# The first norm's weight in PSUM, two weights split on GpSimd, and a wider set of PSUM banks for the attention's transposes

## The chip, the cores and the metric

The kernel runs on one core of a Trainium2 chip. The metric is the device time of one execution in microseconds (us). TensorE (PE in the profile) multiplies matrices and transposes; its weight loads are listed apart (PEld). VectorE (DVE), ScalarE (ACT) and GpSimd (POOL) work elementwise, and SyncE (SP) issues the DMAs here. TensorE writes PSUM, which has eight banks; a bank holds 128 x 512 fp32 values.

## The reference

The reference is a two-layer encoder trunk on 1024 positions of width 1024. Layer 0 mixes tokens by attention with a forget gate, layer 1 by a state-space model; each is followed by a SwiGLU layer, and every part has an RMS norm before and after it. The change touches the very first norm, the projections behind it and the attention. Cut to these:

```python
def rmsnorm(x, gain):
    y = xf * lax.rsqrt(jnp.mean(xf * xf, axis=-1, keepdims=True) + EPS)
    return (y * gain.astype(jnp.float32)).astype(x.dtype)
...
    h = rmsnorm(x, mix_pre_gain[i])
...
def fox_mixer(h, w_in, b_f, q_gain, k_gain, w_out):
    proj = h @ w_in                       # q, k, v, gate, forget logits
    q = rmsnorm(heads(q), q_gain); k = rmsnorm(heads(k), k_gain)
    c = jnp.cumsum(log_sigmoid(f_logit + b_f), axis=1)
    for blk in range(seq_len // Q_BLOCK): # 8 query blocks of 128
        s = q_blk @ k[:k_end].T * scale + c_q - c_k     # 16 heads
        p = softmax(where(mask, s, -inf))
        outs.append(p @ v[:k_end])
    return (o * sigmoid(gate)) @ w_out
```

## The kernel before

Every matrix product is made of three fp32r products: each operand is split into a high part (a cast) and a low part (the difference), and `mm3` (L272 to L274) issues high x high, low x high and high x low. The program is written in an order, and a planner lays out each engine's instructions at compile time from estimated times and priorities; it adds the waits. The order of each engine is then fixed. Tiles in SBUF lie on numbered pages; a ring (`R("x")`) hands its pages out in turn, and a transfer into a page waits until the page's last user is done.

*The start.* SP issues, in this order, block 0 of the input (128 positions x 1024, 512 KB), the norm's weight vector spread over 128 partitions (`gain`, L338, also 512 KB, from one row of 4 KB), blocks 1 to 3, the first two weight tiles of the projections (512 KB each), and blocks 4 to 7. Input blocks use a ring of six pages, so blocks 6 and 7 wait for blocks 0 and 1. `first_norm` takes the blocks in turn. `norm` has ScalarE square and sum the block (L295) and take a root (L299); four small VectorE instructions (L301 to L304) make the reciprocal root. Even blocks are then multiplied by root and weight in one VectorE instruction (L318). Odd blocks are multiplied by the weight on GpSimd (blocks 1 and 3 ahead of the root, L311; blocks 5 and 7 after it, L315) and scaled there (L316). `to_fm` transposes the block on TensorE into two banks (L326, four transposes each), ScalarE casts the high part out of PSUM (L328), VectorE subtracts for the low part (L329). Blocks 0 to 3 are the first half of the positions.

`fox` weaves the rest of the first norm (blocks 4 to 7) with the first head pair's projections in `qkv`: the generators say how much work a step holds, and `weave` takes the one that is behind. The first projection, `qk_proj` of the query weight on the first half, needs blocks 0 to 3 and runs through `fm`, which goes over eight pieces k and yields after four. The first two weights are cast by ScalarE (L253) and subtracted by GpSimd (L254), both behind block 3's scaling; later weights are subtracted by VectorE.

*Attention.* `attend` goes over units: 16 heads, and in each the query blocks 7 down to 0. For a unit, `scores` multiplies into a slot of two PSUM banks (banks 0 and 1, or 2 and 3, in turn by unit; L551, L552). Block qb has (qb + 1) x 128 keys, so blocks 0 to 3 use the slot's first bank alone. VectorE adds the bias and takes the minimum (L555), ScalarE takes the exponential into SBUF (L561). `transposes`, one unit later, transposes the probabilities (L588) in groups of up to four 128 x 128 pieces: a first group for every block (front), a second for blocks 4 to 7 (rear). All groups go to one bank:

```python
PTB = (2,)          # pb() adds 4: PSUM bank 6
...
                p2 = self.pb(PTB, (P, 4, P))
```

ScalarE casts each group (L591) and VectorE subtracts (L592). `values` (L607) multiplies two query blocks at a time. Meanwhile the next head pair's projections (L272 to L274) fill TensorE; `weave` mixes the two streams.

Of the kernel before, what the change touches and what calls it, by code (L numbers as in the profile page):

```python
# [9 lines left out]
F32 = mybir.dt.float32  # L10
# [4 lines left out]
P = 128  # L15
D = 1024
# [10 lines left out]
PROJ = (0, 1)  # L27
# [4 lines left out]
PTB = (2,)  # L32
# [126 lines left out]
class Trunk:  # L159
    def __init__(self, ctx, tc, A, out):  # L160
        self.tc, self.nc, self.A, self.out = tc, tc.nc, A, out
        nc = self.nc
        mk = lambda name, bufs, **k: ctx.enter_context(tc.tile_pool(name=name, bufs=bufs, **k))
        self.cst = mk("cst", 1)
        self.hp = mk("hp", 4)
        self.pp = mk("pp", 1)
        self.sm = mk("sm", 4)
        self.sq = mk("sq", 1)
        self.ps = mk("ps", 1, space=bass.MemoryType.PSUM).tile([P, 8 * 512], F32, name="ps")
        self.nS, self.slots = 0, (0, 2)  # L170
        self.dr = mk("dr", 1, space=bass.MemoryType.DRAM)
        self.uid = 0
        self.R = Rings(tc, self.pp, NPG)
        self.R.set(raw=[0, 1, 2], wh=[3, 4], wl=[5, 6])
        self.B = {}
        c = self.cst
        self.ident = c.tile([P, P], F32, name="ident")
        make_identity(nc, self.ident)
        nc.scalar.preload_act_table_set("sqrt_and_others")
        self.eps = c.tile([P, 1], F32, name="eps")  # L180
        nc.vector.memset(self.eps, EPS)
        self.one = c.tile([P, 1], F32, name="one")
        nc.vector.memset(self.one, 1.0)
        self.lsub, self.proj = nc.vector, PROJ
        self.W, self.loaded, self.cut, self.taken, self.done = [], [], [], 0, {None}

    def nm(self, s):
# [62 lines left out]

    def split(self, h, l, src):
        with self.tc.high_priority(-100):
            self.nc.scalar.copy(h, src)  # L253
            self.lsub.tensor_sub(l, src, f32(h))  # L254

    def take(self, ahead=1):
# [16 lines left out]
        mm(ps, lh, rl, start=False, stop=False)  # L273
        mm(ps, ll, rh, start=False, stop=stop)  # L274

    def fm(self, ps, w, hT, half, step=4):
        wh, wl = w
        h, l = hT[half]
        for k in range(8):
            self.mm3(ps, wh[:, k, :], wl[:, k, :], h[:, k, :], l[:, k, :], k == 0, k == 7)  # L280
            if k % step == step - 1:
                yield 0.65 * step
# [118 lines left out]
        nc.vector.tensor_tensor_scan(z, ones, t1, 0.0, op0=ALU.mult, op1=ALU.add)  # L401
        nc.sync.dma_start(self.csum, z)

    def qk_proj(self, w, hT, hf, st):
        nc = self.nc
        if "p" not in st:
            st["p"] = [self.R(f"p{i}", dt=F32R) for i in st["pages"]]
        ps = self.pb(self.proj)
        yield from self.fm(ps, w, hT, hf)
        X, Y = st[hf] = self.R("pt", (P, 2, 512)), self.R("pt", (P, 2, 512), F32R)  # L410
        with self.tc.high_priority(AHEAD):
            nc.scalar.copy(X[:, 1], ps)
            nc.vector.tensor_mul(X[:, 0], X[:, 1], X[:, 1])
        nc.scalar.copy(Y[:, 0], X[:, 0])
        nc.vector.tensor_sub(Y[:, 1], X[:, 0], f32(Y[:, 0]))
# [54 lines left out]
    def qkv(self, hT, res, hp):  # L470


        v = []
        a, f, b = self.qkp if hp else ([9, 11, 8], [7, 35, 10], [12, 13, 14])
        q, k = dict(pages=a + f[2:]), dict(pages=f[:2])
        self.qkp = a[:2] + f[:1], b, [a[2], f[2], f[1]]
        if hp == 0:
            self.lsub = self.nc.gpsimd
            with self.tc.issue_after(self.poolop.ins):
                wq, wk = self.take(), self.take(0)  # L480
            self.lsub = self.nc.vector
            yield from self.qk_proj(wq, hT, 0, q)
            yield from self.qk_proj(wk, hT, 0, k)
            yield from self.forget_logits(hT)
            yield from self.qk_proj(wq, hT, 1, q)
            self.proj = (0, 1, 2, 3)
            with self.tc.issue_after(self.sqrt.ins):
                self.nc.scalar.preload_act_table_set(LNEXP)
            self.forget_sum()
            yield from self.qk_norm(0, 0, q)  # L490
            yield from self.qk_proj(wk, hT, 1, k)
            wv = self.take()
            yield from self.qk_norm(1, 0, k)
            yield from self.qk_norm(0, 1, q)
        else:
            wk = self.take()
            yield from self.qk_proj(wk, hT, 0, k)
            yield from self.qk_proj(wk, hT, 1, k)
            wq = self.take()
            yield from self.qk_norm(1, 0, k)  # L500
            yield from self.qk_proj(wq, hT, 0, q)
            yield from self.qk_norm(1, 1, k)
            yield from self.qk_proj(wq, hT, 1, q)
            wv = self.take()
            yield from self.qk_norm(0, 0, q)
        last = self.qk_norm(0, 1, q) if hp else self.qk_norm(1, 1, k)
        yield from self.v_proj(wv, hT, v, last)
        res.update(q=q["p"], k=k["p"], v=v)
# [20 lines left out]
    def attend(self, c, o):  # L529
# [3 lines left out]

        nc = self.nc
        units = [(h, qb) for h in range(NH) for qb in reversed(range(8))]
        An, pt, Pt, pv, rs, ri = {}, {}, {}, {}, {}, {}

        def load_bias(h):
            An[h] = self.R("An")
# [2 lines left out]
        def scores(h, qb):  # L542
            qh, ql = c[h // 2]["q"][h % 2 * 2:h % 2 * 2 + 2]
            k = c[h // 2]["k"][h % 2]
            nk = (qb + 1) * P
            qs = slice(qb * P, nk)
            nc.gpsimd.tensor_add(An[h][:, qs], An[h][:, qs], self.cmask)  # L547
            ps = self.S("S")
            for c0 in range(0, nk, 512):
                c1 = min(c0 + 512, nk)  # L550
                nc.tensor.matmul(ps[:, c0:c1], qh[:, qs], k[:, c0:c1], start=True, stop=False)  # L551
                nc.tensor.matmul(ps[:, c0:c1], ql[:, qs], k[:, c0:c1], start=False, stop=True)  # L552
            with self.tc.high_priority(AHEAD):
                m = self.small("mx")
                nc.vector.tensor_tensor_reduce(out=ps[:, :nk], in0=ps[:, :nk], in1=An[h][:, :nk], op0=ALU.add, op1=ALU.min,  # L555
                                               scale=1.0, scalar=3e38, accum_out=m)
            p = Pt[h, qb] = self.R("Pt")
            if h // 2 not in rs:
                rs[h // 2] = self.small("rs", (P, 2, 8))
            r = rs[h // 2][:, h % 2, qb:qb + 1]  # L560
            nc.scalar.activation(p[:, :nk], ps[:, :nk], AF.Exp, bias=m, scale=-1.0, accum_out=r)  # L561
            if h >= NH - 2:
                nc.vector.reciprocal(r, r)
                nc.gpsimd.tensor_scalar(p[:, :nk], p[:, :nk], r, 1.0, op0=ALU.mult, op1=ALU.mult)
# [11 lines left out]
        def transposes(h, qb):  # L576
            j, qq = qb // 2, qb % 2
            if qq:
                ng = (2 * j + 2 + 3) // 4
                pt[h, j] = [(self.R("pth", (P, 4, 256), F32R), self.R("ptl", (P, 4, 256), F32R)) for _ in range(ng)]  # L580
            p = Pt.pop((h, qb))
            for g in range(0, qb + 1, 4):
                n = min(4, qb + 1 - g)
                if g:
                    yield 0.11 * 4
                p2 = self.pb(PTB, (P, 4, P))
                for i in range(n):
                    nc.tensor.transpose(p2[:, i], p[:, (g + i) * P:(g + i + 1) * P], self.ident)  # L588
                th, tl = pt[h, j][g // 4]
                dh, dl = th[:, 0:n, qq * P:qq * P + P], tl[:, 0:n, qq * P:qq * P + P]  # L590
                nc.scalar.copy(dh, p2[:, 0:n])  # L591
                nc.vector.tensor_sub(dl, p2[:, 0:n], f32(dh))  # L592
# [24 lines left out]
        for i in range(len(units) + 3):  # L617
            hp = min(i, len(units) - 1) // 16
            if i < len(units):
                h, qb = units[i]  # L620
# [6 lines left out]
            if 1 <= i <= len(units):  # L627
                h, qb = units[i - 1]
# [5 lines left out]
            if i >= 3 and (i - 3) % 2 == 1:  # L634
                h, qb = units[i - 3]
# [887 lines left out]
def trunk(ctx: ExitStack, tc: tile.TileContext, A, out):  # L1523
    T = Trunk(ctx, tc, A, out)
    nc, R = T.nc, T.R
# [36 lines left out]
    for f in range(8):  # L1562
        T.plan(T.cols(A["s5_w_glu"][0], f * P)[:3] + (("glu",) * 2 if f == 0 else (None,) * 2))
        if f >= 1:
# [7 lines left out]
                gn=[21, 22], ogk=[32])  # L1572
# [9 lines left out]
    hT = T.new_hT()  # L1582
    g0 = []

    def first_norm(tbs, banks):
        for tb in tbs:
            T.norm(xs[tb], g0[0], ys[tb], tb % 2 == 1, R("j") if tb in (1, 3) else None)
            T.to_fm(ys[tb], T.hT_dst(hT, tb), banks)
            yield 1.0

    xs, ys = {}, {}
    R.set(j=[36, 37])
    for tb in range(8):
        xs[tb], ys[tb] = R("x"), R("y")
        nc.sync.dma_start(xs[tb], x0[tb * P:tb * P + P, :])
        if tb == 0:
            g0.append(T.gain("gn", A["mix_pre_gain"][0]))
        if tb == 3:
            T._load(0)
            T._load(1)  # L1600
    T.fox_setup()
    run(first_norm(range(0, 4), (0, 1, 2, 3)))
    T.fox(hT, og_d, first_norm(range(4, 8), (2, 3)), OUT0)
# [9 lines left out]
    ys = {}  # L1613
# [90 lines left out]
```

## Time and profile before

| | |
|---|---|
| median of 3 runs | 2428.12 us (2426.31 to 2430.02) |
| profiled execution | 2426.33 us |
| its span, first to last instruction | 2424.5 us |
| mean granted TensorE clock | 0.995 |
| TensorE busy | 2359.3 us, 97% of the span |
| VectorE, ScalarE, GpSimd busy | 1689.1, 1204.4, 455.2 us |

A row of the timeline reads: start, duration, engine, line of the kernel, operation, output<-input, count; in brackets the idle time of the engine before it and what ended it. A row of a group reads: line, engine, operation, shapes and count | busy us, mean ns of one | idle us before, by releaser. TensorE's instructions are pipelined, and the profile models their ends: matmuls of 512 columns start 0.23 us apart and are listed as 0.39 us long.

### The profile page before, as it was taken

To read this page: it belongs to the slowest core of one execution; us is meant where nothing else is said; L and a number is where in the kernel's file an instruction comes from. 1 tells how busy PE (TensorE), PEld (TensorE's weight loads), DVE (VectorE), ACT (ScalarE), POOL (GpSimd) and SP (SyncE) were. 2 spreads that over 40 slices of the span, in tenths; PEclk is the share of its full clock that TensorE was granted. 3 is DMA by queue.
4 is the path that set the end of the run, shared out by engine and by line. 5 is a ranking of instruction groups with operands and counts; after the bars stand their busy time and mean duration, and the time that the engine had idled before them with its cause. 6 is when DMAs were issued, how large, how long until landed. Compare 5 with 4: busy or idle time off the path is not lost.

```text
span 2424.5 us, 31559 instructions
## 1 busy us (share of the span) xinstructions
PE 2359.3 (97%) x11683; PEld 1938.8 (80%) x11683; DVE 1689.1 (70%) x2684; ACT 1204.4 (50%) x2029; POOL 455.2 (19%) x427
## 2 busy tenths in 40 slices
PE   7999999999999999999999999999999999999997
PEld 5777778777777888888878779888878888888886
DVE  6867776677678967666668686763795656555867
ACT  6766676667646333434564563232453333333334
POOL 4222222222400034545520001410000000000003
PEclk9999999999999999999999999999999999999999
DMA  4121112121243444343688752443424333237874
GB/s 146 48 61 53 49 48 62 53 61 54 87 149 101 121 127 135 117 136 116 204 293 301 270 170 84 135 147 107 135 80 135 107 98 109 92 118 261 284 239 157
DMA packets 252427, 318.23 MB, mean 131 GB/s; under 512 B 34225, under 2 KB 179937, under 8 KB 252273
## 3 DMA queue, kind: packets, MB, share of 16 engines
q1 hardware_dynamic: 252272, 316.23, 40.9%
q8 instruction: 91, 1.49, 0.3%
q14 instruction: 64, 0.52, 0.1%
HBM read 238.46 MB, written 77.72 MB: 130 GB/s over the span
## 4 chain that ended last, share of the span: by engine, by line
PE 74%; DVE 12%; ACT 7%; DMA 3%; issue 3%; POOL 0%; SPq 0%; DVEq 0%; ACTq 0%; POOLq 0%
PE ps L841 33%; PE ps L943 10%; PE ps L272 7%; PE ps L274 7%; PE ps L273 7%; PE ps L588 2%; PE ps L607 2%; DVE ps L555 1%; DMA raw<-in_ffn_w_down_dram 1%; DMA rot_d<-ry 1%; ACT wh L253 1%; PE ps L552 1%; PE ps L551 1%; DVE ptl L592 1%; DVE y L318 1%
## 5 line engine op out<-in xcount | busy, mean ns | idle before, releaser
L841 PE MATMUL ps<-B,ah 128*128 128x512 f32 x1056 | 326.0, 390 | 0.3 <-ACT B L89 0.3
L943 PE MATMUL ps<-wdh,gh 128*128 128x512 f32 x616 | 241.4, 392 | 6.3 <-ACT m L962 3.7
L943 PE MATMUL ps<-wdh,gl 128*128 128x512 f32 x616 | 240.9, 391 | 1.9 <-DVE gl L254 1.9
L943 PE MATMUL ps<-wdl,gh 128*128 128x512 f32 x616 | 240.9, 391 | 0.8 <-DVE wdl L254 0.8
L841 PEld LDWEIGHTS ps<-B,ah 128*128 128x128 f32 x1056 | 198.1, 188 | 42.7 <-ACT B L89 1.2
L841 PE MATMUL ps<-ops,ah 128*128 128x512 f32 x704 | 218.2, 391 | 0.0
L272 PE MATMUL ps<-hT,wh 128*128 128x512 f32 x512 | 207.5, 406 | 1.3 <-DVE pt L429 0.7
L841 PE MATMUL ps<-B,al 128*128 128x512 f32 x528 | 205.4, 389 | 0.0
L273 PE MATMUL ps<-hT,wh 128*128 128x512 f32 x512 | 204.4, 399 | 0.0
L274 PE MATMUL ps<-hT,wl 128*128 128x512 f32 x512 | 202.6, 396 | 0.0
L253 ACT CAST gh<-gr 128x1024 fp32r<-128x1024 f32 (+1 forms) x78 | 81.1, 1040 | 166.4 <-PE ps L943 138.0
L592 DVE TENSOR_TENSOR ptl<-ps,pth 128x512 fp32r<-128x512 f32 x192 | 106.4, 554 | 78.6 <-ACT pth L591 73.6
L254 DVE TENSOR_TENSOR gl<-gr,gh 128x1024 fp32r<-128x1024 f32 (+1 forms) x78 | 98.3, 1262 | 84.0 <-ACT gh L253 83.7
L841 PEld LDWEIGHTS ps<-ops,ah 128*128 128x128 f32 x704 | 131.5, 188 | 28.7 <-issue 1.7
L812 DVE TENSOR_TENSOR al<-raw,ah 128x1024 fp32r<-128x1024 f32 x88 | 117.1, 1333 | 50.5 <-ACT ah L811 50.5
L1655 POOL TENSOR_TENSOR y<-m,s 128x512 f32<-128x512 f32 x4 | 6.5, 1628 | 764.3 <-DVE wdl L254 759.5
L547 POOL TENSOR_TENSOR An<-An,cmask 128x128 f32<-128x128 f32 x128 | 80.2, 629 | 365.8 <-DVE mx L555 332.3
L811 ACT CAST ah<-raw 128x1024 fp32r<-128x1024 f32 x88 | 92.6, 1052 | 101.8 <-PE ps L841 99.4
L943 PEld LDWEIGHTS ps<-wdh,gh 128*128 128x128 f32 x616 | 116.3, 189 | 32.8 <-ACT m L962 4.2
L943 PEld LDWEIGHTS ps<-wdh,gl 128*128 128x128 f32 x616 | 116.2, 189 | 26.9 <-DVE gl L254 2.7
L841 PE MATMUL ps<-ops,al 128*128 128x512 f32 x352 | 136.9, 389 | 0.0
L943 PEld LDWEIGHTS ps<-wdl,gh 128*128 128x128 f32 x616 | 116.3, 189 | 25.5 <-DVE wdl L254 1.5
(358 smaller groups left out, 5867.2 us busy)
## 6 DMA issues: line engine op xcount, KB each, us to landing
raw<-in_ffn_w_down_dram SPq DMA_DIRECT2D x98, 512.0 KB, 5.2
gr<-g_d SPq DMA_DIRECT2D x76, 512.0 KB, 4.4
raw<-in_ffn_w_gate_dram SPq DMA_DIRECT2D x44, 512.0 KB, 4.1
raw<-in_ffn_w_up_dram SPq DMA_DIRECT2D x44, 512.0 KB, 4.8
g_d<-s SPq DMA_DIRECT2D x66, 256.0 KB, 2.2
raw<-in_fox_w_in_dram SPq DMA_DIRECT2D x32, 512.0 KB, 4.3
g_d<-up SPq DMA_DIRECT2D x22, 512.0 KB, 2.7
g_d<-up SPq DMA_DIRECT2D x44, 256.0 KB, 2.9
```

What stands on the lines that cost most here:

```text
L253: self.nc.scalar.copy(h, src)
L254: self.lsub.tensor_sub(l, src, f32(h))
L272: mm(ps, lh, rh, start=start, stop=False)
L273: mm(ps, lh, rl, start=False, stop=False)
L274: mm(ps, ll, rh, start=False, stop=stop)
L547: nc.gpsimd.tensor_add(An[h][:, qs], An[h][:, qs], self.cmask)
L588: nc.tensor.transpose(p2[:, i], p[:, (g + i) * P:(g + i + 1) * P], self.ident)
L592: nc.vector.tensor_sub(dl, p2[:, 0:n], f32(dh))
L811: nc.scalar.copy(h, src)
L812: V.tensor_sub(l, src, f32(h))
L841: nc.tensor.matmul(bank, x[:, k], y, start=start and k == i == 0, stop=True, skip_group_check=True)
L943: nc.tensor.matmul(bank, x[:, j, t], y[:, j], start=start and i == 0, stop=True, skip_group_check=True)
```

## The change

At the start, a 4 KB row of the norm's weight is loaded first. TensorE spreads it: a matmul of a column of ones (one row, `ones`) with the row, twice 512 columns in fp32, writes it to all partitions of PSUM banks 0 and 1 (`gps`). Blocks 0 to 4 and 6 are multiplied by VectorE with the weight from PSUM. Blocks 5 and 7 stay on GpSimd, now with the multiply ahead of the root, and use the old spread tile, which is loaded after block 5. The second weight tile is loaded after block 5 as well. The first two weights are cast and subtracted on GpSimd, no longer behind a norm's instruction. The first projection runs with `apart`: eight high x high products, then eight low x high, then eight high x low, with a yield after each eight.

In attention, the rear groups, and the groups of blocks 2 and 3, go to the second bank of the slot that the unit's own scores used; the front groups of blocks 7 to 4, 1 and 0 stay in bank 6.

```diff
-        self.lsub, self.proj = nc.vector, PROJ
+        self.lsub, self.hcopy, self.proj = nc.vector, nc.scalar.copy, PROJ
...
     def split(self, h, l, src):
         with self.tc.high_priority(-100):
-            self.nc.scalar.copy(h, src)
+            self.hcopy(h, src)
             self.lsub.tensor_sub(l, src, f32(h))
...
+        if apart:
+            for n, (a, b) in enumerate(((wh, h), (wl, h), (wh, l))):
+                for k in range(8):
+                    self.nc.tensor.matmul(ps, a[:, k, :], b[:, k, :], start=n == k == 0, stop=n == 2 and k == 7)
+                yield 0.65 * 8 / 3
+            return
...
         if hp == 0:
-            self.lsub = self.nc.gpsimd
-            with self.tc.issue_after(self.poolop.ins):
-                wq, wk = self.take(), self.take(0)
-            self.lsub = self.nc.vector
-            yield from self.qk_proj(wq, hT, 0, q)
+            self.lsub, self.hcopy = self.nc.gpsimd, self.nc.gpsimd.tensor_copy
+            wq, wk = self.take(), self.take(0)
+            self.lsub, self.hcopy = self.nc.vector, self.nc.scalar.copy
+            yield from self.qk_proj(wq, hT, 0, q, True)
...
             ps = self.S("S")
+            own[h, qb] = self.slots[self.nS % len(self.slots)] + 1
...
-            p = Pt.pop((h, qb))
+            p, b = Pt.pop((h, qb)), own.pop((h, qb))
...
-                p2 = self.pb(PTB, (P, 4, P))
+
+                p2 = self.bank(b, 1, (P, 4, P)) if g or qb in (2, 3) else self.pb(PTB, (P, 4, P))
...
     def first_norm(tbs, banks):
         for tb in tbs:
-            T.norm(xs[tb], g0[0], ys[tb], tb % 2 == 1, R("j") if tb in (1, 3) else None)
+            pool = tb in (5, 7)
+            T.norm(xs[tb], g0[0] if pool else gps, ys[tb], pool, R("j") if pool else None)
...
-    R.set(j=[36, 37])
+    R.set(j=[36, 37], grow=[37])
+
+    gps, grow, v = T.bank(0, 2, (P, D)), R("grow", (1, D)), A["mix_pre_gain"][0]
+    nc.sync.dma_start(grow, bass.AP(tensor=v.tensor, offset=v.offset, ap=[[D, 1], [1, D]]))
+    ones = T.cst.tile([1, P], F32, name="ones")
+    nc.vector.memset(ones, 1.0)
+    for c in (0, 512):
+        nc.tensor.matmul(gps[:, c:c + 512], ones, grow[:, c:c + 512], start=True, stop=True)
     for tb in range(8):
         xs[tb], ys[tb] = R("x"), R("y")
         nc.sync.dma_start(xs[tb], x0[tb * P:tb * P + P, :])
-        if tb == 0:
-            g0.append(T.gain("gn", A["mix_pre_gain"][0]))
         if tb == 3:
             T._load(0)
+        if tb == 5:
             T._load(1)
+            g0.append(T.gain("gn", A["mix_pre_gain"][0]))
```

More of the change, by code (lines that the diff above doesn't have):

```diff
@@ L274, in mm3, with fm @@
         mm(ps, ll, rh, start=False, stop=stop)
-    def fm(self, ps, w, hT, half, step=4):
+    def fm(self, ps, w, hT, half, step=4, apart=False):
         wh, wl = w
         h, l = hT[half]
+        if apart:
[4 more added lines that the diff above has]
+            return
         for k in range(8):
@@ L402, in forget_sum, with qk_proj @@
         nc.sync.dma_start(self.csum, z)
-    def qk_proj(self, w, hT, hf, st):
+    def qk_proj(self, w, hT, hf, st, apart=False):
         nc = self.nc
@@ L408, in qk_proj @@
         ps = self.pb(self.proj)
-        yield from self.fm(ps, w, hT, hf)
+        yield from self.fm(ps, w, hT, hf, apart=apart)
         X, Y = st[hf] = self.R("pt", (P, 2, 512)), self.R("pt", (P, 2, 512), F32R)
@@ L535, in attend @@
         units = [(h, qb) for h in range(NH) for qb in reversed(range(8))]
-        An, pt, Pt, pv, rs, ri = {}, {}, {}, {}, {}, {}
+        An, pt, Pt, pv, rs, ri, own = {}, {}, {}, {}, {}, {}, {}
         def load_bias(h):
```

## The prediction

> **What bounds the kernel now.** I read the page, the busy time by stretch, the timeline of the start, the groups by line, and the waits of the transposes' line with some timeline around them. First the page's span, and busy us, share and instructions by engine:
>
> ```profile
> span 2424.5 us, 31559 instructions
> PE 2359.3 (97%) x11683; PEld 1938.8 (80%) x11683; DVE 1689.1 (70%) x2684; ACT 1204.4 (50%) x2029; POOL 455.2 (19%) x427
> ```
>
> TensorE, busy for 97%, sets the time: whatever starves it at the start or stalls it later is paid in full. The profiled execution took 2426.33 us, 1.8 more than its span and 1.8 under the median of 2428.12; sums made on its rows are taken off the median. A measurement of this kernel can tell about 0.2% (4.9 us) from no change.
>
> By stretch (length, then busy us of TensorE, its weight loads, VectorE, ScalarE, GpSimd):
>
> ```profile
> 0.00:21.00 21.00, 7.95 (x33) 6.39 (x33) 11.95 (x35) 14.44 (x27) 11.31 (x15) 1.00 0.93 298
> 21.00:45.00 24.00, 24.00 (x115) 17.32 (x115) 15.81 (x33) 11.77 (x24) 12.76 (x8) 1.00 0.18 49
> 157.00:235.00 78.00, 76.42 (x413) 61.87 (x414) 56.16 (x97) 54.05 (x104) 18.69 (x25) 1.00 0.19 56
> ```
>
> Two places matter. Until 21 us TensorE mostly waits; from there to 45 it has no idle time, so an earlier first projection moves the rest with it. In attention its idle looks small, but busy time is modelled to a matmul's end and hides late starts; I come back to that.
>
> **The start.** The timeline (start, us, engine, line; brackets are idle time and releaser):
>
> ```profile
> 0.74 0.38 SPq L1595 DMA_DIRECT2D x<-in_x_dram  x1
> 4.48 1.06 ACT L295 ACTIVATE y<-x 128x1024 f32<-128x1024 f32 x1 [2.46 <-DMA x<-in_x_dram]
> 6.74 1.28 DVE L318 SCALAR_TENSOR_TENSOR y<-x,rr,gn 128x1024 f32<-128x1024 f32 x1
> 7.71 1.06 ACT L295 ACTIVATE j<-x 128x1024 f32<-128x1024 f32 x1 [1.76 <-DMA x<-in_x_dram]
> 8.17 1.94 PE L326 MATMUL ps<-ident,y 128*128 128x128 f32 x8 [8.17 <-DVE y L318]
> 12.21 2.34 POOL L311 TENSOR_TENSOR y<-x,gn 128x1024 f32<-128x1024 f32 x1
> 12.76 2.87 DVE L318 SCALAR_TENSOR_TENSOR y<-x,rr,gn 128x1024 f32<-128x1024 f32 x1
> 18.71 4.71 POOL L254 TENSOR_TENSOR wl<-raw,wh 128x1024 fp32r<-128x1024 f32 x2
> 18.80 1.97 PE L326 MATMUL ps<-ident,y 128*128 128x128 f32 x8 [1.15 <-POOL y L316]
> 20.87 1.29 DVE L329 TENSOR_TENSOR hT<-ps,hT 128x512 fp32r<-128x512 f32 x2 [0.32 <-ACT hT L328]
> 20.89 1.22 PE L272 MATMUL ps<-hT,wh 128*128 128x512 f32 x2
> ```
>
> Block 0 reaches ScalarE at 4.48, block 1 only at 7.71: the spread weight and block 1 land between, 3.2 us for two transfers, 1.6 each. Block 2's multiply on VectorE takes 2.87 beside a GpSimd multiply; block 0's, alone, 1.28. A subtraction whose one input is in PSUM (L329, 1.29 for two) isn't slowed by the GpSimd work running from 18.71. So a multiply that takes its weight from PSUM should cost about 1.28 beside GpSimd, too.
>
> ```profile
> L302 DVE RECIPROCAL rr<-rt 128x1 f32<-128x1 f32 x8 | 1.1, 152 | 0.3 <-ACT rt L299 0.3
> L303 DVE TENSOR_SCALAR tt<-vv,rr 128x1 f32<-128x1 f32 x8 | 2.0, 270 | 0.1
> L304 DVE TENSOR_SCALAR rr<-tt,rr 128x1 f32<-128x1 f32 x8 | 1.5, 208 | 0.1
> L316 POOL TENSOR_SCALAR y<-y,rr 128x1024 f32<-128x1024 f32 x4 | 5.3, 1334 | 3.2 <-DVE rr L304 3.1
> L441 POOL CAST p<-p 64x512 fp32r<-64x512 f32 x64 | 53.0, 828 | 76.9 <-ACT p L437 48.5 <-issue 25.5
> 22.54 0.43 PE ps L274
> 24.76 0.23 PE ps L274
> 36.42 0.87 PE ps L326 x8
> ```
>
> *Removed:* the 512 KB spread ahead of block 1 (1.6 us) and ScalarE's two weight casts. *Added ahead:* one 4 KB row; its issue puts block 0 0.4 us back (block 0's own takes 0.38), so blocks land at about 4.9, 6.5, 8.1 and 9.7. ScalarE's squares, 1.06 each, keep up: block 3's ends near 10.8. VectorE takes 2.1 per block: 0.15, 0.27 and 0.21, one more small one like the first, and the multiply's 1.28, which blocks 1 and 3 left to GpSimd before. Block 0's multiply starts at 4.9 + (6.74 - 4.48) = 7.2 and ends at 8.4; three more end at 14.6, or at 17.2 when the subtractions of two blocks (2 x 1.29) are planned between. From the start of a block's transposes to the first projection the trace has 20.89 - 18.80 = 2.1. So TensorE starts its projection between 16.7 and 19.3; I take the middle, 18.0, as subtractions of earlier blocks come first in program order but the last can wait: the first projection now asks for the high parts first. **Gain 2.9 us, ends 1.6 and 4.2.**
>
> *The weight in PSUM.* No row shows a one-row matmul of 512 fp32 columns. Bounds: not under 2 x 0.43 (a projection matmul at the start's slow pace) and, by the transposes at 1.94 for eight of 128 columns, 0.24 x 4 x 2 = 1.9. The row lands between 1.9 us (half of block 0's 3.7) and 3.7 after 0.74, so the weight stands at 3.5 to 6.4 and block 0 needs it at 7.2: nothing to pay. The Trainium skill (FP8 and Floating Point Precision, TensorE Precision Notes) counts four passes for true fp32: an estimate of 2 x 4 x 0.43 = 3.4, ready by 7.9 at the worst, 0.7 late, which would leave a gain of 2.2 and a sum of 2413.9; no row here shows it.
>
> *GpSimd.* It gets two casts: by L441's 828 ns for half the elements per lane 1.7 each (by L316's scaling, 1.3); with the subtractions (4.71) 8.1 us. Blocks 5 and 7 keep 2 x (2.4 + 1.3) = 7.4. In all 15.5 from weight 0's landing near 11.3, with a pause of 0.7 for weight 1: done by 28. Its last piece is block 7, which TensorE wanted at 36.42, and would want at 33.5: covered by 6 us. Should weight 1 come last of all, the second projection (18.0 + 12 slow matmuls x 0.43 + 12 x 0.23 + two blocks' transposes at 0.87, about 28) still finds it. Weight 1 and the spread weight now queue behind block 5, seven and eight transfers of 1.6 after 4.9, and land near 16.1 and 17.7; only blocks 5 and 7 read the spread. SP's later loads (blocks 6 and 7, the small gains, the forget weight) come no later than before, as the bytes are the same. Emitting the first projection in three runs of eight changes no instruction. It asks for block 4 after eight matmuls instead of twelve: at 18.0 + 8 x 0.43 = 21.4, when VectorE, with blocks 0 to 4 and four blocks' subtractions (8.4 + 4 x 2.1 + 4 x 1.29 = 22.0), may be 0.6 late, within the ends above.
>
> **The transposes' bank in attention.** Per unit (head, query block) the front group of up to four transposes, and for query blocks 4 to 7 a rear group, all write bank 6. Each group must be cast by ScalarE and subtracted by VectorE before the next may write. The change leaves fronts of blocks 7 to 4 and blocks 1, 0 there, and puts rears and blocks 3, 2 into the second bank of the unit's own scores. Idle time before the transposes (us, times), and who waited for the subtraction:
>
> ```profile
>   DVE ptl L592: 48.3, 121
>   ACT Pt L561: 3.9, 10
>   PEld ps L588: 39.9, 99
>   PE ps L588: 8.5, 22
> ```
>
> ```profile
> 202.58 0.39 PE L272 MATMUL ps<-hT,wh 128*128 128x512 f32 x1
> 202.80 0.69 DVE L592 TENSOR_TENSOR ptl<-ps,pth 128x512 fp32r<-128x512 f32 x1
> 203.55 0.33 PE L588 MATMUL ps<-ident,Pt 128*128 128x128 f32 x1 [0.58 <-DVE ptl L592]
> ...
> 590.18 0.40 PE L272 MATMUL ps<-hT,wh 128*128 128x512 f32 x1
> 591.12 0.33 PE L588 MATMUL ps<-ident,Pt 128*128 128x128 f32 x1 [0.54 <-DVE ptl L592]
> ```
>
> That is the rear group of block 4, first and last of six such pairs: the matmul before starts at 202.58, the next could at 202.81 (0.23 a step), it starts at 203.55, just after the subtraction: 0.74 lost, though the row says 0.58 idle. The modelled end hides 0.39 - 0.23 = 0.16. So the 22 waits that show on TensorE cost 8.5 + 22 x 0.16 = 12.0 us. The other 77 of the weight loads' 99 are hidden by modelled ends and cost 0 to 0.16 each: 12.0 to 24.3 in all. I take 12.0, the part that is seen, since a new order will leave some waits. What is late next? For these groups the exponentials are long done:
>
> ```profile
> 265.79 0.60 PE L588 MATMUL ps<-ident,Pt 128*128 128x128 f32 x4
> 266.43 0.59 ACT L591 CAST pth<-ps 128x512 fp32r<-128x512 f32 x1 [1.65 <-PE ps L588]
> 267.16 0.91 ACT L561 ACTIVATE Pt<-ps,mx 128x768 f32<-128x768 f32 x1
> 268.33 0.55 PE L588 MATMUL ps<-ident,Pt 128*128 128x128 f32 x3
> 270.13 0.56 DVE L592 TENSOR_TENSOR ptl<-ps,pth 128x384 fp32r<-128x384 f32 x1
> 270.34 0.22 PE L551 MATMUL ps<-p,p 128*128 128x128 f32 x1
> 270.74 0.66 PE L588 MATMUL ps<-ident,Pt 128*128 128x128 f32 x4
> ```
>
> Block 5's exponential ends at 268.07; its front starts at 270.74, behind block 6's rear (268.33, subtracted until 270.69). Fronts of consecutive units are then alone in their bank; TensorE has projection work to fill in. VectorE, 56 of 78 us, and ScalarE, 54, don't bind. The 3.9 on the exponential stays. **Gain 12.0; ends 0 (each wait is replaced) and 20 (the hidden ones at 0.1).**
>
> **Sum:** 2428.1 - 2.9 - 12.0 = 2413.2.
>
> **Rivals.**
> *A, the waits only move.* Instruction order is fixed at compile time, by estimated times; that order already leaves groups waiting 0.74 and units on exponentials. A new order may trade bank waits for others. Only the start is won: 2425.2. For it: 3.9 us of exponential waits; against: the fill.
> *B, slower: the scores wait for the second bank.* In the rows above block 4's scores write their second bank at 270.34 while block 6's rear is subtracted until 270.69. With the rear in that bank, these scores, and so the reduction and the exponential behind them, would wait. Places: blocks 5 and 4, 32 in all. If the rears stay where they are, a full cast and subtraction, 0.59 + 0.69 = 1.3 each, 41 us: 2428.1 - 14.9 + 41 = 2454; it undoes the forecast's gain from 14.9/32 = 0.47 each, and makes the kernel slower by 0.2% from 0.62. Against: the rear is free to start right behind its front (265.79 + 0.60 for block 6), at 266.4 and not 268.33. The Trainium skill (PSUM — Partial Sum Buffer, PSUM bank collisions raise a hardware error) speaks for it: accesses are to be guarded by bank, whatever the addresses. No row shows this pair yet.
> *C, more:* the freed groups also let values and scores move up, and the start reaches its good end: 20 + 4 gives 2404.
>
> **Chances.** The forecast 0.58, own range 2407 to 2419; A 0.19, B 0.08, C 0.15. A reaches from 2419 to 2431. Range 2404 to 2426. Faster than 2423.3: forecast, C and a third of A, 0.78; slower than 2433: B, 0.08; the rest 0.14.
>
> **What would show it.** First projection matmul at 17 to 19.5; four VectorE multiplies near 1.28; the transposes' idle on the subtraction under 5 of 48.3 us, rears starting within 1.5 us of fronts; attention ending 11 to 16 us earlier. Wrong if waits on exponentials or of scores on subtractions grow by as much, or if block 3's norm is late behind subtractions.

## Result: 18.4 us less, 0.9925 of the time before

| | before | after |
|---|---|---|
| median | 2428.11 us of 4 runs | 2409.74 us of 4 runs (2406.97 to 2412.92) |
| profiled execution, span | 2426.33, 2424.5 us | 2412.92, 2411.0 us |
| ratio of the runs | | 0.9925 (95%: 0.9907 to 0.9942) |

The forecast was 2413.2, with a range of 2404 to 2426. The page of the changed kernel, span and busy us by engine:

```profile
span 2411.0 us, 31475 instructions
PE 2352.0 (98%) x11687; PEld 1946.3 (81%) x11687; DVE 1683.7 (70%) x2687; ACT 1197.0 (50%) x2027; POOL 450.9 (19%) x425
```

TensorE still sets the time; its share rose from 97% to 98%. The busy time of a stretch of attention, first of before, then of after (length, then TensorE, weight loads, VectorE, ScalarE, GpSimd, each with its count; last the granted clock, the DMA share and GB/s):

```profile
80.00:612.00 532.00, 519.96 (x2815) 421.06 (x2813) 386.33 (x671) 369.69 (x712) 129.59 (x175) 1.00 0.18 53
```

```profile
80.00:612.00 532.00, 523.71 (x2896) 437.04 (x2897) 395.92 (x702) 373.21 (x732) 138.44 (x187) 1.00 0.19 56
```

TensorE's busy time differs by 3.75 us, but in the same 532 us it starts 81 instructions more. The count tells the gain; the busy time, with its modelled ends, hides most of it.

To place the gain I take five moments from each trace: the start of the first projection's first matmul, of attention's first transposes, of the first gate and up matmul (behind attention and the output projection), of the first down matmul of layer 0 and of the last down matmul of all (us; "length" is from the second to the third):

```
kernel            project.  transp.  gate/up  length   down      last
before             20.89     79.6    757.68   678.1   1203.04   2414.41
after              19.40     77.4    739.11   661.8   1186.94   2400.36
start alone        19.98     77.8    756.45   678.6   1201.86   2417.36
attention alone    20.91     79.6    741.70   662.1   1187.05   2398.09
```

By gate and up 18.6 us are won: 2.2 before attention, 16.4 in it and the output projection. Behind that the code is the same, and the difference between the two profiled executions wanders by some 4 us (16.1 at the first down, 14.1 at the end of this one, the longest of the four after runs). The medians, over several executions, differ by 18.4.

**The start, after** (start, us, engine, line; brackets: idle time and releaser):

```profile
2.49 3.75 PE L1608 MATMUL ps<-grow,ones 1*128 1x512 f32 x4 [2.49 <-DMA grow<-in_mix_pre_gain_dram]
4.91 1.06 ACT L302 ACTIVATE y<-x 128x1024 f32<-128x1024 f32 x1 [2.90 <-DMA x<-in_x_dram]
6.29 1.04 ACT L302 ACTIVATE y<-x 128x1024 f32<-128x1024 f32 x1
7.24 1.28 DVE L325 SCALAR_TENSOR_TENSOR y<-x,rr,ps 128x1024 f32<-128x1024 f32 x1
9.25 1.28 DVE L325 SCALAR_TENSOR_TENSOR y<-x,rr,ps 128x1024 f32<-128x1024 f32 x1
10.45 1.51 DVE L336 TENSOR_TENSOR hT<-ps,hT 128x512 fp32r<-128x512 f32 x2
10.60 1.04 POOL L253 CAST wh<-raw 128x1024 fp32r<-128x1024 f32 x1 [7.92 <-DMA raw<-in_fox_w_in_dram]
11.72 2.36 POOL L254 TENSOR_TENSOR wl<-raw,wh 128x1024 fp32r<-128x1024 f32 x1
12.97 1.29 DVE L336 TENSOR_TENSOR hT<-ps,hT 128x512 fp32r<-128x512 f32 x2
14.41 1.28 DVE L325 SCALAR_TENSOR_TENSOR y<-x,rr,ps 128x1024 f32<-128x1024 f32 x1
16.10 2.37 POOL L254 TENSOR_TENSOR wl<-raw,wh 128x1024 fp32r<-128x1024 f32 x1
16.24 1.27 DVE L325 SCALAR_TENSOR_TENSOR y<-x,rr,ps 128x1024 f32<-128x1024 f32 x1
```

The weight stands in PSUM at 6.24, before block 0's multiply wants it at 7.24. Block 1 reaches ScalarE at 6.29 instead of 7.71. All four multiplies take 1.28, that of block 3 (16.24) beside GpSimd's second L254 too. But between the second and the third stand the subtractions of blocks 0 and 1 (10.45, 12.97).

**Attention's transposes, after** (idle time before them by releaser, us and times; then who waited for the subtraction L600; then idle before the scores, L558):

```profile
  DVE ptl L600: 9.3, 19
  POOL Pt L571: 9.2, 17
  ACT Pt L568: 4.5, 9
```

```profile
  PEld ps L558: 9.3, 22
  PEld ps L596: 6.6, 13
  PE ps L596: 2.8, 6
  PE ps L558: 1.4, 6
```

```profile
  DVE ptl L600: 10.6, 28
```

The transposes' 48.3 us on the subtraction are 9.3. In their place the scores wait 10.6 for it, which they never did before. GpSimd's scaling of the probabilities (L571), done for the last two heads only, is the next late piece there, 2.3 before and 9.2 now, all of it between 597 and 638 us. These lists count some waits twice: one that shows on the weight load and on the matmul behind it has an entry under each. The 121 of before are 99 waits, 22 of which show on both; the 28 at the scores are 22, with 6 on both. A stretch of the timeline that shows both sides:

```profile
254.25 1.03 PE L596 MATMUL ps<-ident,Pt 128*128 128x128 f32 x8
255.14 1.08 ACT L599 CAST pth<-ps 128x512 fp32r<-128x512 f32 x2
255.88 1.28 DVE L600 TENSOR_TENSOR ptl<-ps,pth 128x512 fp32r<-128x512 f32 x2
...
262.98 0.56 DVE L600 TENSOR_TENSOR ptl<-ps,pth 128x384 fp32r<-128x384 f32 x1
263.02 0.39 PE L558 MATMUL ps<-p,p 128*128 128x512 f32 x1
263.59 0.19 PEld L558 LDWEIGHTS ps<-p,p 128*128 128x128 f32 x1 [0.38 <-DVE ptl L600]
263.59 0.33 PE L558 MATMUL ps<-p,p 128*128 128x128 f32 x1
```

At 254.25 front and rear of block 7 run as eight transposes on end, where the rear used to wait for the front's subtraction. In 56 of the 64 units with a rear it starts 0.4 to 1.4 us after the front's start; before it was 2.0 to 4.6 in all of them. At 263.59 block 4's scores for the second bank wait until block 6's rear is subtracted (263.54): rival B's pair, 0.34 behind the earliest start (263.02 + 0.23).

### The profile page after: what moved, and what is told of

The parts are those of the page before. It is cut to its first block, busy times and chain, and to the rows that moved or that the text cites. A ratio compares the mean times of both kernels' runs of the same rounds, so it can differ in the third digit from the quotient of the medians.

```text
span 2411.0 us, 31475 instructions
## 1 busy us (share of the span) xinstructions
PE 2352.0 (98%) x11687; PEld 1946.3 (81%) x11687; DVE 1683.7 (70%) x2687; ACT 1197.0 (50%) x2027; POOL 450.9 (19%) x425
## 4 chain that ended last, share of the span: by engine, by line
PE 72%; DVE 13%; ACT 5%; DMA 4%; issue 4%; POOL 3%; SPq 0%; DVEq 0%; ACTq 0%; POOLq 0%
PE ps L849 29%; PE ps L951 11%; PE ps L272 7%; PE ps L273 7%; PE ps L274 7%; PE ps L615 2%; PE ps L596 2%; DMA raw<-in_ffn_w_down_dram 2%; PE ps L558 1%; DVE ps L562 1%; PE ps L559 1%; DVE al L820 1%; DVE y L325 1%; POOL s5w L1213 1%; DVE ptl L600 1%
## 5 line engine op out<-in xcount | busy, mean ns | idle before, releaser
L272 PE MATMUL ps<-hT,wh 128*128 128x512 f32 x504 | 200.7, 398 | 1.1 <-DVE pt L436 0.6
L273 PE MATMUL ps<-hT,wh 128*128 128x512 f32 x504 | 197.5, 392 | 0.0
L254 DVE TENSOR_TENSOR gl<-gr,gh 128x1024 fp32r<-128x1024 f32 (+1 forms) x78 | 97.1, 1246 | 87.0 <-ACT gh L253 87.0
L600 DVE TENSOR_TENSOR ptl<-ps,pth 128x512 fp32r<-128x512 f32 x192 | 102.5, 551 | 56.6 <-ACT pth L599 55.9
L553 POOL TENSOR_TENSOR An<-An,cmask 128x128 f32<-128x128 f32 x128 | 77.8, 609 | 342.3 <-DVE mx L562 310.7
```

What stands on the lines that cost most here:

```text
L272: mm(ps, lh, rh, start=start, stop=False)
```

## Experiments

All ratios are to the kernel before on the same chip, with 95% intervals.

**1. The two halves of the change.** One kernel keeps the new start and has `p2 = self.pb(PTB, (P, 4, P))` again; the other has only the attention edit.

> The changed kernel's start with the old attention: every transposes group back in bank 6. Bank theory (the start gives what the two traces show at the first attention transposes, 2.2 us, and the bank the rest): 2425.5 to 2426.5, the transposes' idle on the subtraction back near 48 us. Rival, the two parts need each other (an earlier start also shifts the weaving, so that attention gains without the banks): below 2420.

> The old start with the changed kernel's attention banks. Bank theory: the whole attention gain without the start's, 18.4 - 2.2 = 16 us, so 2411 to 2413, about 2.05 us gained in each of the six middle head pairs. Rival, the parts need each other: above 2417.

Start alone: 2423.77 us, 0.9990 (0.9981 to 0.9999). Attention alone: 2412.13, 0.9944 (0.9932 to 0.9956). The gains by medians, 3.6 and 15.3, add up to 18.9 against 18.4 together; by the ratios they are 2.4 and 13.6 against 18.2. By the moments above they are 1.2 and 16.0 at gate and up, against 18.6. So within some 2 us the edits don't help or hurt each other, and three quarters or more of the gain are the attention's. Kernels with the same start code put the first projection anywhere from 19.25 to 19.98, as the blocks land a little earlier or later: differences under 0.7 us there mean nothing. Counted from the start of block 0's transposes, though, it comes after 10.73 or 10.74 us in all six of them.

**2. Which groups go where.** The attention edit varied, the new start kept:

```diff
-  p2 = self.bank(b, 1, (P, 4, P)) if g or qb in (2, 3) else self.pb(PTB, (P, 4, P))
rears alone:
+  p2 = self.bank(b, 1, (P, 4, P)) if g else self.pb(PTB, (P, 4, P))
rears of blocks 7 and 6 stay in bank 6:
+  p2 = self.bank(b, 1, (P, 4, P)) if (g and qb < 6) or qb in (2, 3) else self.pb(PTB, (P, 4, P))
fronts of blocks 1 and 0 in the second bank too:
+  p2 = self.bank(b, 1, (P, 4, P)) if g or qb < 4 else self.pb(PTB, (P, 4, P))
front and rear both in the unit's second bank:
+  p2 = self.bank(b, 1, (P, 4, P)) if qb > 1 else self.pb(PTB, (P, 4, P))
```

> The changed kernel, but only the rear groups leave bank 6; the groups of blocks 3 and 2 go back to it. Bank theory: the waits that were largest before belong to rears (6b, 5b, 4b) and to the group behind one (5a); blocks 3 and 2 then have predecessors at some distance, so nearly the whole gain stays: 2409 to 2413. Rival, the two blocks count as much as the rears (4 of 12 groups moved): 2414 or more.

> The changed kernel, but the rears of blocks 7 and 6 go back to bank 6, so that no scores write a bank that a rear has used just before (blocks 5 and 4 of the scores no longer wait for a subtraction). Theory that bank 6 is what counts: about 5 us of the gain lost (6b 2.6 and 5a 3.1 us before), 2413 to 2416. Rival B, the scores' new waits (10.6 us at the weight loads, 1.4 shown on TensorE itself) cost as much as these rears gain: 2408 to 2411, not worse than the changed kernel.

> The changed kernel, with blocks 1 and 0 moved to their units' own second banks as well, so that only fronts of blocks 7 to 4 use bank 6. Bank theory: the 9.3 us of idle on the subtraction that are left before the transposes belong to these neighbours; half of it is hidden, so 1 to 4 us are gained: 2406 to 2409. Rival A, what is left moves to the exponential and to GpSimd's scaling: 2409 to 2412.

> The changed kernel, but front and rear of a unit (blocks 7 to 2) both go to the second bank of the unit's own scores, so that a rear again waits for its own front's subtraction, while groups of different units are apart. Bank theory, group by group: the rears' waits come back (6b 2.6, 5b 2.6, 4b 4.3 us in the kernel before, over the six repeating head pairs), the waits of 5a, 1 and 0 stay away: a head pair takes 76.5 to 77.2 us instead of 75.45, the time 2417 to 2422. Rival, any second bank will do (the new plan gains, not the pairing): 2408 to 2413.

Measured, with TensorE's idle time on the subtraction before transposes and before scores, and the length as above:

```
                      us       ratio (95%)              transp.  scores  length
before                                                   48.3      0     678.1
start alone          2423.77   0.9990 (0.9981-0.9999)    49.0      0     678.6
rears of 7, 6 stay   2410.95   0.9935 (0.9922-0.9948)    23.2      0     664.2
fronts of 1, 0 too   2410.09   0.9927 (0.9914-0.9940)     8.2     16.7   664.4
rears alone          2412.24   0.9937 (0.9925-0.9949)    11.7     10.4   664.2
attention alone      2412.13   0.9944 (0.9932-0.9956)     9.6     10.5   662.1
after                2409.74   0.9925 (0.9907-0.9942)     9.3     10.6   661.8
front, rear in one   2428.81   1.0005 (0.9996-1.0014)    22.9     33.6   682.9
```

The length follows the sum of the two idle columns: from before to after 28.4 us of idle less and 16.4 us of length, 0.58 per us; from before to the last row 8.2 more and 4.8 longer, 0.59. The three variants between lie at 0.53 to 0.59. That is a ratio of these kernels, not the price of a wait: some waits stand in the columns twice, and with the idle time on GpSimd's scaling added the ratios scatter from 0.3 to 0.8. Times alone can't order the middle five, whose intervals overlap. The lengths part them in two: the eight kernels of this study with the change's attention, whatever their start, lie between 661.5 and 662.1, the three variants at 664.2 to 664.4. Moving the fronts of blocks 1 and 0 too misses its 2406 to 2409: the transposes' idle time falls by 1.1 only, and the scores' grows by 6.1.

The last row is rival B at work, and slower than both of its expectations, which had left the scores out. With a unit's front and rear in the same bank, the rear again follows the front's cast and subtraction, and the scores of two units later wait for it. Its idle before transposes, and who waited for the subtraction at the scores:

```profile
  DVE ptl L600: 22.9, 62
```

```profile
  PEld ps L558: 20.5, 21
  PE ps L558: 13.1, 12
```

Of 21 waits 12 show on TensorE, 1.1 us each by the list and 1.3 from start to start, the full cast and subtraction of 1.3 that the prediction gave rival B; and all of attention's gain is gone. In the change the front stays out, so the rear runs right behind it and its subtraction ends in time, but for 22 waits, which cost 3.9 us in all from start to start. Leaving the rears of blocks 7 and 6 in bank 6 takes those waits away and brings 37 of the old ones back: the length grows by 2.5. Rival B's wait is there, then, but costs less than what it replaces.

**3. The weight in PSUM or in SBUF.** All six VectorE multiplies stay, but take the weight from the spread tile, loaded right behind block 0 as in the kernel before; the row, the ones and the two matmuls go.

> The changed kernel, but the weight is spread by DMA into SBUF behind block 0 as before, and all VectorE multiplies read it there; no matmul into PSUM. Theory of the contention and of the queue (the reason for PSUM): block 1 again reaches ScalarE near 7.7 us, multiplies that run beside GpSimd's weight work take 2 to 2.9 us instead of 1.28, and the first projection starts 1.5 to 3 us later, at 21 to 22.4. Rival, the weight's place does not matter, since the subtractions are the bound: 19.4 to 20.4.

One run: 2413.25 us. Projection at 22.03, transposes at 80.6, gate and up at 742.08: 2.6, 3.2 and 3.0 later than after, and later than before by 1.1 and 1.0 at the first two. Its start:

```profile
7.72 1.06 ACT L302 ACTIVATE y<-x 128x1024 f32<-128x1024 f32 x1 [1.75 <-DMA x<-in_x_dram]
13.19 1.28 DVE L325 SCALAR_TENSOR_TENSOR y<-x,rr,gn 128x1024 f32<-128x1024 f32 x1
13.26 3.44 POOL L254 TENSOR_TENSOR wl<-raw,wh 128x1024 fp32r<-128x1024 f32 x1
18.38 1.71 DVE L325 SCALAR_TENSOR_TENSOR y<-x,rr,gn 128x1024 f32<-128x1024 f32 x1
18.95 2.04 POOL L253 CAST wh<-raw 128x1024 fp32r<-128x1024 f32 x1
```

Block 1 comes at 7.72 again, 1.4 later than in after, as the theory of the queue has it. Two VectorE multiplies beside GpSimd behave differently: the one at 13.19 keeps its 1.28 and GpSimd's subtraction takes 3.44, the one at 18.38 takes 1.71. How much of the 2.6 is the queue and how much contention isn't shown, because VectorE's order differs too: block 2's transposes start at 14.54, 1.2 earlier than in after, but block 3's multiply stands behind block 2's subtractions (16.31 and 17.16), which in after come behind it. With the weight in SBUF, loaded behind block 0, the start's other edits together are thus a loss of 1; the weight in PSUM, with its early row, is what pays.

**4. The other two edits of the start.** The first projection without `apart`; and the two high parts cast by ScalarE again.

```diff
-            yield from self.qk_proj(wq, hT, 0, q, True)
+            yield from self.qk_proj(wq, hT, 0, q)
```

```diff
-            self.lsub, self.hcopy = self.nc.gpsimd, self.nc.gpsimd.tensor_copy
+            self.lsub = self.nc.gpsimd
```

> The changed kernel, but its first projection isn't cut in three runs of eight: each step takes high by high, low by high and high by low as everywhere else. The prediction priced the three runs at nothing beyond letting the projection begin on the high parts. Theory: begun the old way, the second and third matmul need weight 0's low part and block 3's first low part, so the first projection waits for the subtraction of block 3 and starts, or stalls behind its first matmul, 0.7 to 1.5 us later than the 19.40 of the changed kernel; first transposes of attention 0.5 to 1.5 later than 77.4; total 0 to 2 more. Rival (the three runs matter more, because weight 0's low part, made on GpSimd, is the late piece): 2 to 4 us later. Rival (no matter): within 0.3.

> The changed kernel with the high parts of the two first weights cast by ScalarE again, GpSimd only subtracting. Theory (ScalarE has room: at the start it waits for the blocks): its two casts of about 1.1 each fall between the casts of the transposes, and GpSimd ends 2 us earlier; the first projection moves by under 0.7 us either way, the first transposes of attention by under 0.7, total within 2 us of the changed kernel. Rival (ScalarE binds at the start, since block 2's root stands behind block 0's casts there already): each cast pushes a root or a cast of the chain back, first projection 1 to 2.2 us later, and the total 1 to 2 more.

Without `apart`: 2413.14, 0.9942 (0.9928 to 0.9955); projection at 19.31, transposes at 77.4, gate and up at 739.20, all within 0.1 of after. TensorE does stall behind the first matmuls, 1.04 us by the weight loads' row:

```profile
19.31 1.02 PE L272 MATMUL ps<-hT,wh 128*128 128x512 f32 x2
20.82 0.19 PEld L273 LDWEIGHTS ps<-hT,wh 128*128 128x128 f32 x1 [1.04 <-DVE hT L336]
```

and yet nothing is later by the time attention begins. The "no matter" rival holds by these moments; the theory of 0.5 to 1.5 us doesn't. The median is 3.4 above after's, but the intervals overlap, and up to gate and up the profile shows no loss. With ScalarE's casts: 2410.63, 0.9926 (0.9910 to 0.9942); projection at 19.80, inside the 19.25 to 19.98 of unchanged starts, but behind a ScalarE that casts the second weight first:

```profile
16.50 1.04 ACT L253 CAST wh<-raw 128x1024 fp32r<-128x1024 f32 x1
17.44 2.26 ACT L335 CAST hT<-ps 128x512 fp32r<-128x512 f32 x4
...
19.80 2.47 PE L283 MATMUL ps<-hT,wh 128*128 128x512 f32 x5 [0.73 <-ACT hT L335]
```

Attention's transposes start at 78.8 (76.3 to 77.8 in kernels with the change's start), gate and up at 740.60. Counted from block 0's transposes, the projection comes after 11.53 us, 0.8 later than the 10.73 of all kernels with the change's start. So ScalarE's casts do cost 0.8 at the projection, a little over the theory's 0.7 and under the rival's 1 to 2.2, and 1 to 1.5 by the later moments; the medians are too coarse to show it.

**5. Why the projection came at 19.4 and not at 18.0.** First, all subtractions of blocks 0 to 3 behind block 3's multiply:

```diff
+            if tb >= 4: T.to_fm(ys[tb], T.hT_dst(hT, tb), banks)   # blocks 0 to 3: after the loop
...
+            with self.tc.issue_after(self.dveop.ins) if late else nullcontext():
                 nc.vector.tensor_sub(l, ps, f32(h))
```

> The changed kernel, with the subtractions of the first four blocks held behind block 3's multiply on VectorE (and the four norms written ahead of the four transposes). It tests the step of the prediction that put the first projection between 16.7 us (no subtraction ahead) and 19.3 (those of two blocks ahead); the changed kernel has it at 19.40, with two blocks' ahead. Theory that the plan's subtractions cost the start's missing microsecond: the first projection at 16.7 to 17.5, 2 us earlier, and 1 to 2 us less in all if the low parts come in time: 2408. Rival, ScalarE's order (block 2's root behind block 0's cast) or the low parts hold it: first projection after 18.5, no gain.

2408.18 us, 0.9914 (0.9898 to 0.9930), an interval that overlaps with after's. The multiplies now end at 14.83, but the projection starts at 18.68, not by 17.5:

```profile
13.55 1.28 DVE L325 SCALAR_TENSOR_TENSOR y<-x,rr,ps 128x1024 f32<-128x1024 f32 x1
14.75 3.07 DVE L337 TENSOR_TENSOR hT<-ps,hT 128x512 fp32r<-128x512 f32 x5
15.49 3.32 PE L333 MATMUL ps<-ident,y 128*128 128x128 f32 x16 [3.05 <-DVE hT L337]
```

Block 2's multiply had ended at 12.9; its transposes wait until 15.49 for a subtraction. `first_norm` has four banks, and blocks 0 and 1 hold them until they are subtracted. So two more banks, unused at that time:

```diff
-    run(first_norm(range(0, 4), (0, 1, 2, 3)))
+    run(first_norm(range(0, 4), (0, 1, 2, 3, -2, -1)))
```

> The kernel with all eight subtractions behind block 3's multiply, and six PSUM banks instead of four for the first norm's transposes (the two added ones are free until attention). Theory (in the kernel with the late subtractions, blocks 0 and 1 hold the four banks until their subtractions, so block 2's transposes start at 15.49 and not behind its multiply, which ends at 12.9): with two more banks block 2's transposes start at 13 to 13.5, block 3's right behind its multiply at 14.9 to 15.2, and the first projection 2.1 later, at 17.0 to 17.6 instead of 18.68; the first transposes of attention and the first gate and up matmul move by the same 1.1 to 1.7; total 2406 to 2408, ratio near 0.991. Rival (VectorE's queue binds: eight subtractions of 0.65 from 14.8 end at 20.0, and block 4's multiply comes behind them): the first projection starts by 17.6 but TensorE then stalls ahead of the low parts or of block 4, and the first transposes of attention stay at 76.2 within 0.5; total as before, 2408.

2411.39 us, 0.9930 (0.9917 to 0.9942): a miss. The wait moved twice.

```profile
12.93 1.97 PE L333 MATMUL ps<-ident,y 128*128 128x128 f32 x8 [0.50 <-DVE y L325]
15.49 1.59 PE L333 MATMUL ps<-ident,y 128*128 128x128 f32 x8 [0.58 <-DVE hT L337]
19.16 3.08 PE L283 MATMUL ps<-hT,wh 128*128 128x512 f32 x8 [2.09 <-DVE hT L337]
```

Block 2 is on time at 12.93. Block 3 comes on block 0's banks and waits 0.6; and the projection's own bank is one that block 3 has, so it waits 2.1 until that is subtracted. This profile has a second handicap behind that start: the granted clock is 0.50 from 20 to 22 us, and the projection's first eight matmuls take 3.08 us, against 2.06 in the next kernel. The last kernel therefore subtracts one half of block 0 early, in a gap of VectorE, and hands the six banks out in another order:

```diff
+            if tb == 1: T.to_fm(ys[0], T.hT_dst(hT, 0), banks, ks=(0,))
...
+    run(first_norm(range(0, 4), (2, 3, 0, 1, -2, -1)))
```

> As the kernel with six banks, but only the subtraction of block 0's first half stands ahead of block 2's multiply; the other seven follow block 3's, that of block 0's second half first; the six banks are handed out so that block 3's transposes come on block 0's banks, and the first projection's bank is one that block 1 gives back second. Theory (what kept the start at 18.7 and 19.2 in the two kernels with late subtractions was banks held by groups not yet subtracted: block 3's 0.6 and the projection's own 2.1 in the six-bank kernel): multiplies end at 8.4, 10.4, 12.9 and 14.9 as there, block 3's transposes start at 14.9 to 15.2, the first projection 2.1 later, 17.0 to 17.5; attention's first transposes 74.6 to 75.6 instead of 77.8; total 2406 to 2409 with the scatter of the stages behind attention, ratio 0.990 to 0.992. Rival (VectorE's queue): the projection starts by 17.5 but stalls ahead of its seventeenth matmul or of block 4's transposes, whose multiply now ends after 20.5, and attention's first transposes come no earlier than 76.2. Rival (ScalarE): block 4's square and the roots stand ahead of block 3's casts, and the projection starts after 18.2.

2406.00 us (2404.84 to 2408.29), 0.9911 (0.9895 to 0.9928). Projection at 17.97, attention's transposes at 75.2, gate and up at 737.14: 1.4, 2.2 and 2.0 earlier than after.

```profile
13.58 3.71 PE L333 MATMUL ps<-ident,y 128*128 128x128 f32 x16 [1.17 <-DVE y L325]
13.99 1.28 DVE L325 SCALAR_TENSOR_TENSOR y<-x,rr,ps 128x1024 f32<-128x1024 f32 x1
16.26 1.04 ACT L302 ACTIVATE j<-x 128x1024 f32<-128x1024 f32 x1
17.30 1.06 ACT L335 CAST hT<-ps 128x512 fp32r<-128x512 f32 x2
17.97 2.06 PE L283 MATMUL ps<-hT,wh 128*128 128x512 f32 x8 [0.68 <-issue]
```

No transposes and no projection wait for a bank any more. Block 3's transposes end at 17.29 and its cast starts at 17.30, so block 5's square (16.26 to 17.30; only blocks 5 and 7 are squared into `j`) held up the cast of its first half by up to 0.9. Block 3's multiply is 0.44 late as well (13.99 for 13.55). Together they more than cover the 0.5 by which the projection misses 17.5. The bank theory is borne out; a small part of the ScalarE rival is there as well, with block 5's square in the place of block 4's. This is the best kernel of the study. Its time alone doesn't separate it from after, as the intervals overlap; the moments do.

## Why the prediction was right, step by step

*The start: 2.9, ends 1.6 and 4.2.* First projection 1.5 earlier, at 19.40 just outside the worse end of 19.3; first transposes 2.2 earlier; start alone 3.6 by medians, 2.4 by the ratio. The single prices held: blocks at 4.9 and 6.3 (said 4.9 and 6.5), multiplies 1.28 beside GpSimd, the weight there before it was needed. On the weight's spreading, the Trainium skill (FP8 and Floating Point Precision, TensorE Precision Notes) with its four passes had given an estimate of 3.4 us; the row has 3.75, so the trace agrees with it to about a tenth; the upper of my bounds from rows, 1.9, was too low. GpSimd's cast took 1.04 and not 1.7: a 64-partition cast of 512 was a bad yardstick for it. The step that failed is the choice of 18.0, the middle, on the ground that the last subtractions can wait. They weren't put off: those of two blocks stand ahead of block 2's multiply, the worse end of that same sum. One of the prediction's own signs of being wrong, block 3's norm late behind subtractions, thus came: its multiply ended at 17.51, past the 17.2 of the sum's worse end. Putting them off showed a resource that the prediction had not counted, the banks that an unsubtracted block holds.

*Attention: 12.0, ends 0 and 20.* Measured 16.4, inside the ends; the mechanism is the one named, but the sum's make-up was not. I took all of the visible waits as gone and none of the hidden ones. Both can be measured in the traces, from start to start: what a matmul starts later than the median step behind a matmul of the same kind. Before, the 22 visible waits lost 12.0, as the prediction had worked out, and the 77 hidden ones 6.5, 0.08 each. Of the 99, there remain 13 with 6 visible, and 22 with 6 visible are new at the scores; these 35 lose 8.6, of which 6.0 visible. So the waits on the subtraction account for 18.5 - 8.6 = 9.9 of the 16.4. The other 6.5 lie at starts for which the lists name no such wait; that they go with the banks is shown by the kernels above, how they do is not.

*The total.* The start was put 0.7 to 1.4 too high by the moments and attention 4.4 too low. The errors have opposite signs, and part of the attention's gain is one that no term stood for: that the sum came within 3.5 us is in part luck.

*"Idle on the subtraction under 5 of 48.3"* was 9.3. Rears within 1.5 of their fronts: 56 of 64; six of the others are block 7's, at 3.2. Attention ending 11 to 16 us earlier: 18.6 at gate and up, past that sign, of which 16.4 in attention.

*Rivals.* A fell: the new waits (10.6 at the scores, 6.9 more on GpSimd's scaling) are less than the 39 removed. B's place was right, its price was right where a rear is kept waiting (1.1 to 1.3 each, the kernel with front and rear in one bank), and so was the reason against it in the change. The Trainium skill (PSUM — Partial Sum Buffer, PSUM bank collisions raise a hardware error) wants accesses guarded by bank; the row at 263.59 and the 22 waits of scores show that guard and what it costs, 3.9. C, 2404, wasn't reached.

## What to carry to other kernels

A bank or buffer that several groups share is a queue: give each group the one whose last reader ends earliest, and write down, bank by bank, who must have read before who may write, because a wait taken away at one bank can show up at the next. Price an engine's waits by the start times of its instructions, not by its busy time, and mind that the line's idle list can hold a wait twice. A vector that is needed on all partitions can be spread by a matmul with a row of ones (here two, from a 4 KB row), which takes a 512 KB transfer out of the start.

## What was not expected of the hardware

In the kernel with the weight in SBUF, GpSimd's subtraction that starts 0.07 behind a VectorE multiply takes 3.44 us instead of 2.36, while the multiply keeps its 1.28; in the kernel before, where GpSimd's multiply had started first (12.21 against 12.76), it was VectorE that paid (2.87 for 1.28). The Trainium skill (SBUF — State Buffer, Who interferes with whom) says that a VectorE instruction with two inputs in SBUF and a GpSimd one that reads SBUF contend for a shared pair of ports, and that the later one blocks until the earlier is done: 13.19 + 1.28 + 2.36 is 16.83, and the subtraction ended at 16.70, so the trace agrees. And a GpSimd cast of 128 x 1024 to fp32r takes 1.04 us, as long as ScalarE's.
